# Loading gamma through GpSimd's DMA queue in a grouped instance norm

## Chip, cores, metric

The kernel runs on one core of a Trainium2 chip. The metric is the device time in microseconds (us), as a median over executions.

## The reference

```python
def setup_inputs():
    B, G, C_per_g, H, W = 4, 8, 16, 256, 256
    return {"x": np.random.randn(B, G, C_per_g, H, W).astype(np.float32),
            "gamma": np.random.randn(G, C_per_g).astype(np.float32)}

def reference(x, gamma):
    mu = x.mean(axis=(3, 4), keepdims=True)
    var = ((x - mu) ** 2).mean(axis=(3, 4), keepdims=True)
    x_norm = (x - mu) / np.sqrt(var + 1e-5)
    return (x_norm * gamma[None, :, :, None, None]).astype(np.float32)
```

Each of 512 channels of 65,536 values is normalized by its own mean and variance, and scaled by one of 128 gammas. That is 134 MB in and 134 MB out.

## The kernel before

The input is cut into 32 tiles of 128 rows by 8192 floats (4 MB). A tile holds 16 channels, each on 8 rows. There are six tile buffers ("slots"). Loads are issued by SyncE's queue, save two of the first six, and stores by ScalarE's queue.

```python
    def load(u, queue):
        queue.dma_start(out=slots[u % AHEAD][:], in_=xv[u])

    g_row = singles.tile([1, G * C], F32, name="g_row")
    for u in range(AHEAD):                                  # AHEAD = 6
        if u == 1:
            nc.scalar.dma_start(out=g_row[:], in_=gv[None, :])
        load(u, nc.scalar if u in (1, 3) else nc.sync)
    # ... cut: GpSimd writes eps, a one and the averaging matrix navg ...
    nc.vector.tensor_copy(out=g_rep[:], in_=g_row[:]...)     # each gamma eight times
    # ... cut: 8 small matmuls turn g_rep into columns ...
    nc.vector.tensor_copy(out=g_col[:], in_=g_ps[:])

    for u in range(U):                                      # U = 32
        t = slots[u % AHEAD]
        nc.vector.reduce_sum(out=st[:, u, 0:1], in_=t[:], axis=AX.X)
        square = nc.scalar.activation(out=junk[:], in_=t[:], func=ACTF.Square,
                                      accum_out=st[:, u, 1:2])
        # ... cut: matmul with navg, variance, root, reciprocal, times g_col ...
        nc.vector.tensor_scalar(out=t[:], in0=t[:], scalar1=ps[:, 0:1],
                                scalar2=scale[:, u : u + 1], op0=ALU.add, op1=ALU.mult)
        nc.scalar.dma_start(out=ov[u], in_=t[:])
        if u + AHEAD < U:
            load(u + AHEAD, nc.sync)
```

In the built program the transfers of SyncE and ScalarE have eight completion semaphores (counters that a transfer raises when it has landed) in turn. A transfer must wait until the last one on its semaphore has landed. In VectorE's order of instructions the copy of gamma stands in front of everything that it does with the first tile.

## Time and profile before

| | before |
|---|---|
| time, median of 3 | 627.18 us (626.75 to 627.25) |
| span of the profiled run | 625.2 us |
| mean DMA rate | 429 GB/s |

The busiest engines and how long a store takes to land, from the page's parts 1, 5 and 6. In part 5 the columns are busy time and mean ns of one, then the idle time before it and what ended it:

```profile
PE 21.4 (3%) x80; PEld 19.5 (3%) x80; DVE 443.2 (71%) x162; ACT 238.8 (38%) x98; POOL 1.3 (0%) x9
L103 DVE TENSOR_REDUCE st<-xt 128x1 f32<-128x8192 f32 x32 | 277.9, 8684 | 111.2 <-DMA xt<-in_x_dram 111.2
L126 DVE TENSOR_SCALAR xt<-xt,ps,scale 128x8192 f32<-128x8192 f32 x32 | 145.6, 4550 | 1.2
out_dram<-xt ACTq DMA_DIRECT2D x32, 4096.0 KB, 67.1
```

VectorE is the busiest engine but idles 111 us for loads. A store takes 67 us to land although 4 MB occupy the DMA engines for 9.6 us: it stands in a queue. Engines that wait for transfers, and transfers that wait for each other, point to the DMA engines as the bound.

### The profile page before, as it was taken

Reading aid. Unit: us, or ns where it says so; the run is one execution under the profiler, and the core shown is the slowest. Engines: PE = TensorE matmul, PEld = TensorE weight load, DVE = VectorE, ACT = ScalarE, POOL = GpSimd, SP = SyncE. Lnnn points to the kernel's source line nnn. Section 1 sums busy time; section 2 is a strip of 40 time slices with the busy share of each in tenths; the row PEclk is TensorE's granted clock in tenths of the full one; section 3 lists DMA queues with packets and bytes.
Section 4 is the critical chain, followed back from the end, with each engine's and each line's share of the span. In section 5 each row is a group of like instructions: output and inputs, shape, how many; then the busy total and the mean of one; then the engine's idle time right before and its main releaser. Section 6 shows DMA issues by size and latency. Waiting matters only on the chain.

```text
span 625.2 us, 626 instructions
## 1 busy us (share of the span) xinstructions
PE 21.4 (3%) x80; PEld 19.5 (3%) x80; DVE 443.2 (71%) x162; ACT 238.8 (38%) x98; POOL 1.3 (0%) x9
## 2 busy tenths in 40 slices
PE   2000000000000000000000000000000000000000
PEld 2000000000000000000000000000000000000000
DVE  0699999998867668676687766776667867668620
ACT  0444444444444224443244432344423443224400
POOL 0000000000000000000000000000000000000000
DMA  8999999999999999999999999999999999999998
GB/s 369 436 417 424 434 436 436 436 436 437 434 436 434 426 426 430 434 436 436 436 434 434 436 434 434 430 426 430 434 436 436 436 432 434 436 436 434 426 426 365
DMA packets 9220, 268.46 MB, mean 429 GB/s; under 512 B 1025, under 2 KB 1026, under 8 KB 1026
## 3 DMA queue, kind: packets, MB, share of 16 engines
q10 hardware_dynamic: 4898, 142.61, 52.8%
q1 hardware_dynamic: 4320, 125.83, 46.8%
q14 instruction: 2, 0.02, 0.0%
HBM read 134.22 MB, written 134.22 MB: 429 GB/s over the span
## 4 chain that ended last, share of the span: by engine, by line
another core or an unknown queue 64%; DMA 16%; DVE 13%; SPq 1%; PE 1%; issue 0%; ACT 0%
DMA xt<-in_x_dram 9%; DVE st L103 8%; DMA out_dram<-xt 7%; DVE xt L126 4%; SPq L48 1%; PE ps L112 1%; ACT std L117 0%; DVE nvar L113 0%; DVE rstd L121 0%; DVE scale L123 0%
## 5 line engine op out<-in xcount | busy, mean ns | idle before, releaser
L103 DVE TENSOR_REDUCE st<-xt 128x1 f32<-128x8192 f32 x32 | 277.9, 8684 | 111.2 <-DMA xt<-in_x_dram 111.2
L104 ACT ACTIVATE junk<-xt 128x8192 uint8<-128x8192 f32 x32 | 225.0, 7030 | 272.2 <-DMA xt<-in_x_dram 229.0
L126 DVE TENSOR_SCALAR xt<-xt,ps,scale 128x8192 f32<-128x8192 f32 x32 | 145.6, 4550 | 1.2
L117 ACT ACTIVATE std<-nvar,eps_t 128x1 f32<-128x1 f32 x32 | 9.4, 294 | 79.6 <-DVE nvar L113 79.6
L112 PE MATMUL ps<-st,navg 128*128 128x2 f32 x64 | 17.9, 349 | 568.0 <-DVE st L103 568.0
L112 PEld LDWEIGHTS ps<-st,navg 128*128 128x128 f32 x64 | 16.0, 312 | 569.8 <-issue 569.8
L113 DVE TENSOR_SCALAR nvar<-ps 128x1 f32<-128x1 f32 x32 | 9.2, 287 | 23.8 <-PE ps L112 23.8
L121 DVE RECIPROCAL rstd<-std 128x1 f32<-128x1 f32 x32 | 5.3, 164 | 11.6 <-ACT std L117 11.6
L104 ACT ACTIVATION_READ_ACCUMULATOR junk<-xt 128x1 f32 x32 | 6.0, 186 | 0.0
L123 DVE TENSOR_TENSOR scale<-rstd,g_col 128x1 f32<-128x1 f32 x32 | 5.1, 159 | 1.1
L84 PE MATMUL g_ps<-one,g_rep 1*128 1x1 f32 x16 | 3.5, 346 | 2.9 <-DVE g_rep L79 2.9
L84 PEld LDWEIGHTS g_ps<-one,g_rep 1*128 1x128 f32 x16 | 3.5, 325 | 2.9 <-POOL navg L68 2.9
L90 DVE COPY g_col<-g_ps 128x8 f32<-128x8 f32 x1 | 0.2, 166 | 3.7 <-PE g_ps L84 3.7
L74 ACT ACT_TABLE_LOAD x1 | 1.3, 1283 | 2.2 <-issue 2.2
L79 DVE COPY g_rep<-g_row 1x1024 f32<-1x1024 f32 x1 | 0.7, 681 | 2.1 <-DMA g_row<-in_gamma_dram 2.1
L64 POOL TENSOR_SCALAR_AFFINE_SELECT navg<-navg 128x128 f32<-128x128 f32 x1 | 0.4, 403 | 0.1
L68 POOL TENSOR_SCALAR_AFFINE_SELECT navg<-navg 128x128 f32<-128x128 f32 x1 | 0.4, 398 | 0.1
L63 POOL MEMSET navg<- 128x128 f32 x1 | 0.2, 220 | 0.0
L74 ACT ACTIVATE root_eps<-eps_t 128x1 f32<-128x1 f32 x1 | 0.2, 203 | 0.0
L147 POOL MEMSET const-bfloat16-1.0<- 128x1 bf16 x1 | 0.1, 101 | 0.0
L147 POOL MEMSET const-uint8-127<- 128x1 uint8 x1 | 0.1, 101 | 0.0
L147 POOL MEMSET const-float32-0.0<- 128x1 f32 x1 | 0.1, 98 | 0.3 <-issue 0.3
(3 smaller groups left out, 0.3 us busy)
## 6 DMA issues: line engine op xcount, KB each, us to landing
out_dram<-xt ACTq DMA_DIRECT2D x32, 4096.0 KB, 67.1
xt<-in_x_dram SPq DMA_DIRECT2D x30, 4096.0 KB, 33.8
xt<-in_x_dram ACTq DMA_DIRECT2D x2, 4096.0 KB, 33.3
g_row<-in_gamma_dram ACTq DMA_DIRECT2D x1, 0.5 KB
```

The costliest lines, as they stand in the source:

```text
L48: queue.dma_start(out=slots[u % AHEAD][:], in_=xv[u])
L74: nc.scalar.activation(out=root_eps[:], in_=eps_t[:], func=ACTF.Sqrt)
L79: nc.vector.tensor_copy(out=g_rep[:], in_=g_row[:].rearrange("o (n k) -> o n k", n=NG).unsqueeze(3).to_broadcast([1, NG, K, S]),)
L84: nc.tensor.matmul(out=g_ps[:, n : n + 1], lhsT=g_rep[:, n].rearrange("o k s -> o (k s)"), rhs=one[:], start=True, stop=True,)
L103: nc.vector.reduce_sum(out=st[:, u, 0:1], in_=t[:], axis=AX.X)
L104: square = nc.scalar.activation(out=junk[:], in_=t[:], func=ACTF.Square, accum_out=st[:, u, 1:2],)
L112: nc.tensor.matmul(out=ps[:], lhsT=navg_w, rhs=st[:, u], start=True, stop=True)
L113: nc.vector.tensor_scalar(out=nvar[:, u : u + 1], in0=ps[:, 0:1], scalar1=ps[:, 0:1], scalar2=ps[:, 1:2], op0=ALU.mult, op1=ALU.add,)
L117: nc.scalar.activation(out=std[:, u : u + 1], in_=nvar[:, u : u + 1], func=ACTF.Sqrt, bias=eps_t[:], scale=-1.0,)
L121: nc.vector.reciprocal(out=rstd[:, u : u + 1], in_=std[:, u : u + 1])
L123: nc.vector.tensor_mul(out=scale[:, u : u + 1], in0=rstd[:, u : u + 1], in1=g_col[:, g : g + 1],)
L126: nc.vector.tensor_scalar(out=t[:], in0=t[:], scalar1=ps[:, 0:1], scalar2=scale[:, u : u + 1], op0=ALU.add, op1=ALU.mult,)
```

## The change

The intent: 64 data transfers are a multiple of the eight semaphores, 65 are not. If gamma's load goes to GpSimd's queue, which has semaphores of its own, the data fill the eight evenly.

```diff
     g_row = singles.tile([1, G * C], F32, name="g_row")
+    nc.gpsimd.dma_start(out=g_row[:], in_=gv[None, :])
     for u in range(AHEAD):
-        if u == 1:
-            nc.scalar.dma_start(out=g_row[:], in_=gv[None, :])
         load(u, nc.scalar if u in (1, 3) else nc.sync)
```

## The prediction

> **What bounds the kernel now.** I read the share of busy time first, then the forty slices, then the stretches, and only then the waits. The header and the slices of the profile page:
>
> ```profile
> span 625.2 us, 626 instructions
> DMA  8999999999999999999999999999999999999998
> GB/s 369 436 417 424 434 436 436 436 436 437 434 436 434 426 426 430 434 436 436 436 434 434 436 434 434 430 426 430 434 436 436 436 432 434 436 436 434 426 426 365
> DMA packets 9220, 268.46 MB, mean 429 GB/s; under 512 B 1025, under 2 KB 1026, under 8 KB 1026
> ```
>
> The reader is to see that the DMA row is full from the second slice to the second last, while VectorE is at 71% and ScalarE at 38% of the span. The best slices move 436 GB/s. A slice is 625.2 / 40 = 15.63 us. Against 436 in each slice the forty rates fall short by 262 in sum (67 in the first, 71 in the last, 31 in the third and fourth together, 93 in all the rest), and 262 / 436 x 15.63 us = 9.4 us. So a change that made the transfers perfect from the first instant to the last could win 9.4 us, 1.5%. The stretches say where those are:
>
> ```profile
> 0.00:1.80 1.80, 0.00 (x0) 0.00 (x0) 0.00 (x0) 0.00 (x0) 1.07 (x9) 1.00 0.00 0
> 1.80:20.00 18.20, 3.54 (x16) 3.48 (x16) 0.85 (x2) 1.49 (x2) 0.22 (x1) 1.00 1.04 432
> 20.00:62.00 42.00, 1.67 (x6) 1.50 (x6) 38.15 (x15) 22.25 (x9) 0.00 (x0) 1.00 1.00 424
> 62.00:156.00 94.00, 3.36 (x12) 3.02 (x12) 85.73 (x31) 44.51 (x18) 0.00 (x0) 1.00 1.01 434
> 156.00:560.00 404.00, 11.71 (x42) 10.52 (x42) 290.79 (x105) 155.75 (x63) 0.00 (x0) 1.00 1.00 433
> 560.00:622.00 62.00, 1.12 (x4) 1.00 (x4) 27.69 (x10) 14.83 (x6) 0.00 (x0) 1.00 1.01 435
> 622.00:625.20 3.20, 0.00 (x0) 0.00 (x0) 0.00 (x0) 0.00 (x0) 0.00 (x0) 1.00 0.07 31
> ```
>
> The last two numbers of a row are the share of the sixteen DMA engines and GB/s. No byte moves before 1.8 us, the engines are full until 622.0, and the last 3.2 us are the tail. Between, the share is 1.00 or more in every stretch: no stage waits for an engine or a semaphore with idle transfers.
>
> The timeline shows the start, which is all that the change touches by intent:
>
> ```profile
> 0.80 1.90 SPq L48 DMA_DIRECT2D xt<-in_x_dram  x4
> 0.80 0.53 ACTq L54 DMA_DIRECT2D g_row<-in_gamma_dram  x1
> 1.37 0.84 ACTq L48 DMA_DIRECT2D xt<-in_x_dram  x2
> 2.06 0.68 DVE L79 COPY g_rep<-g_row 1x1024 f32<-1x1024 f32 x1 [2.06 <-DMA g_row<-in_gamma_dram]
> 6.46 0.17 DVE L90 COPY g_col<-g_ps 128x8 f32<-128x8 f32 x1 [3.72 <-PE g_ps L84]
> 20.32 8.69 DVE L103 TENSOR_REDUCE st<-xt 128x1 f32<-128x8192 f32 x1 [13.70 <-DMA xt<-in_x_dram]
> ```
>
> VectorE is done with gamma at 6.6 us and then idles 13.7 us for the first tile. And the semaphores, from the view of the load line and of the store line:
>
> ```profile
> L48 SPq EVENT_SEMAPHORE  x26: 28/18926/19472, 64.4 to 530.0; - x26
> L130 ACTq EVENT_SEMAPHORE  x27: 17/17/17, 74.9 to 573.2; - x27
> DMA to landing us min/median/max: 29.0/67.1/67.3
> ```
>
> These are minimum, median and maximum in ns, then the landing times of stores in us. The 26 waits on SyncE take about 19 us each: a load waits until the store of its slot has landed, which is real data dependence at the pace of the DMA. The 27 waits that ScalarE executes ahead of its stores take 17 ns, all of them: they were always met before ScalarE came to them.
>
> **What the Trainium skill says.** First, "DMA: Bandwidth & Descriptors", section "Issuing engines are not separate DMA queues": transfers started from scalar, sync or gpsimd run on the same 16 DMA engines, and starting them from several saves only the sequencer's issue time. The trace agrees as to the full engines; the issue time at stake is the 0.53 us above. Second, "Perfetto Trace Analysis", section "Roofline": a single active core is bounded by its 16 DMA engines at about 435 GB/s in sum; the 434 to 436 of most slices is that. Third, the DMA page's section "Why a DMA increments its semaphore by 16 and not by 1": a transfer whose slowest dimension is 128 rows spreads over 16 engines and each posts one increment, while a small one on fewer engines has the sequencer write the rest. The packet count agrees: 64 data transfers x 16 = 1024, and 1025 packets are under 512 B, so gamma had one data packet and one increment; its issue took 0.53 us against 0.34 us for a later store. Fourth, its section "Latency and other measured facts": first byte about 0.6 us on the HWDGE path (sync, scalar), about 1 us on the SWDGE path (gpsimd). No transfer from GpSimd is in this trace.
>
> **The change part by part.**
>
> One, ScalarE loses one issue, 0.53 us. Its two loads start at 0.80 instead of 1.37 us. Nothing is won: SyncE's first load was issued at 0.80 already and 4 MB occupy the engines for 4.19 / 0.436 = 9.6 us, so they have work from 1.8 us on either way. There is a small loss: the first tile shares the engines with the second, and loses its 0.57 us of lead, so it may land up to 0.6 us later (20.9 instead of 20.3). VectorE works tiles off in 14.93 us (35.34 to 50.27 in the chain of waits), the DMA needs 19.35 us for a load and a store, so this shift is swallowed by 157 us, where VectorE first waits for a tile again. Cost at the end: 0.
>
> Two, GpSimd gains one issue ahead of its memsets. I have no duration for it here. My estimate is that gamma lands at 3 to 8 us: issue at 0.80, the 1.3 us that gamma took on ScalarE's queue (0.80 to 2.06), the 0.4 us or more that the page's first byte is later, and some packets of 32 KB to wait behind (16 engines at 436 GB/s are 27 GB/s each, 1.2 us for one packet). The deadline: the first reduction at 20.32 must be preceded by the 0.68 us copy, the 3.7 us of small matmuls and the 0.17 us copy, 4.6 us in sum, so gamma may land as late as 15.7 us and nothing moves. The constants that GpSimd makes after it come later by its issue; the mean matrix is first needed at 29.1 us and eps at 20 us.
>
> Three, the semaphores. The built program of both shows which waits change. Before, the data transfers began at semaphore 1, gamma having 0; after the start, loads had the even ones and stores the odd ones, and the period is eight. Afterwards they begin at 0, loads have odd and stores even, and the period is eight still. In both, a store waits besides its data for the store four before it, and a load for the load four before it. The stores are spaced 4 x 19.35 = 77.4 us and land in at most 67.3 us: met 10 us early. Loads, at a median of 33.8 us, are met 43 us early. What vanishes is one wait, of the seventh load for gamma's semaphore, met 62 us before that load was issued at 64.5. What is new is that the third store waits for the fourth load, which is on the chip by then. Removed 0, added a few times 17 ns on ScalarE, which idles 62% of the span.
>
> Four, bytes. Gamma's 512 B split 16 ways are 32 small packets (16 of data, 16 of increments) instead of 2: two more short ones per engine, well under 0.1 us.
>
> Sum: 0 + 0 + 0 + under 0.1 us, off the path that sets the end save the last. The kernel stays at 1.8 us start, 620 us of full transfers, 3.2 us tail.
>
> **The rivals.** (a) The author's hope: uneven semaphores cost waits. Against it are the 17 ns waits and the DMA share of 1.00; for it only the slices of 417 and 424, where stores begin, and 426 to 430 later. If those came from a semaphore, the engines would idle in them, which they don't. All of it would be worth at most (31 + 93) / 436 x 15.63 = 4.4 us: 622.7. (b) Gamma lands late, since GpSimd's queue takes turns with two full queues, or its first issue is slow. If it passes 15.7 us by X, the first store at 35.4 us moves by X. But the six first loads alone fill the DMA to 1.8 + 6 x 9.6 = 59.4 us, so the engines would run dry only with X over 24 us, a landing past 40 us, and 2% (12.5 us) needs past 52. (c) The third queue costs something outside the transfers, in the start or the final drain: the time is 1.7 us above the span in the profiled run (626.89 against 625.2), and 1 or 2 us more would make 628 to 629. Nothing in the trace speaks for it; the program before declares GpSimd's queue too. (d) The first two loads, now started together, interleave otherwise and the rate in the first 60 us shifts: 424 against 434 there is 1 us in 42, either way.
>
> **Range and chances.** The prediction is the time before, 627.1 us. The three runs before spread by 0.5 us, and executions agree within 0.3%, 1.9 us. With (c) and (d) each worth about 1 us I take 625.7 to 628.4. Faster by 2% would need 614.6, under what the bytes allow at 436 GB/s (268.46 / 0.436 = 615.7 us), so only another chip or a mistake of mine gives it: 1%. Slower by 2% needs (b) at its worst or something unseen: 1%. Within 2%: 98%.
>
> **What would show it.** The DMA share stays at 1.00 from 1.8 to 622 us, and the mean at 429 GB/s. Packets are some 9250, with 1056 or so under 512 B, and a small third queue appears. ScalarE's first load is issued at 0.80 us. The copy of gamma starts at 3 to 8 us, and the first reduction at 20.3 to 20.9 us. SyncE's waits stay at 19 us and ScalarE's at 17 ns. I would be wrong if the first reduction started after 25 us, if a stretch had idle DMA, if ScalarE's waits ahead of stores took microseconds, or if the gap between time and span grew past 3 us.

## The result

| | before | after |
|---|---|---|
| median of 6 | 627.05 us | 626.92 us |
| range | 626.75 to 627.38 | 626.73 to 627.32 |
| profiled span | 625.2 us | 625.2 us |

The ratio is 0.9999, with a 95% interval of 0.9986 to 1.0012: the same. (A ratio here is the mean time of one kernel's fast runs over that of the other's fast runs of the same rounds, so not quite the ratio of the medians.)

The page of the changed kernel, its rates, packets and the new queue:

```profile
span 625.2 us, 627 instructions
GB/s 369 436 403 436 436 436 436 436 426 432 434 434 436 424 434 436 436 434 436 436 421 434 434 434 432 432 434 436 436 434 436 436 419 434 434 436 432 432 434 369
DMA packets 9251, 268.46 MB, mean 429 GB/s; under 512 B 1057, under 2 KB 1057, under 8 KB 1057
q0 software_dynamic: 32, 0.00, 0.0%
g_row<-in_gamma_dram POOLq DMA_DIRECT2D x1, 0.5 KB, 9.3
```

The mean rate is 429 GB/s again. The dips below 436 have moved to other slices but add up to nearly the same (265 against 262). Queue q0 is GpSimd's, with gamma's 32 small packets. The last line says that gamma took 9.3 us to land.

The start in the timeline (start us, duration us, engine, line, what; in brackets the idle time before it and what ended it):

```profile
0.81 0.89 ACTq L48 DMA_DIRECT2D xt<-in_x_dram  x2
1.29 0.61 POOL L52 DMA_DIRECT2D g_row<-in_gamma_dram  x1 [0.78 <-POOLq L146]
10.64 0.68 DVE L78 COPY g_rep<-g_row 1x1024 f32<-1x1024 f32 x1 [10.64 <-DMA g_row<-in_gamma_dram]
15.05 0.17 DVE L89 COPY g_col<-g_ps 128x8 f32<-128x8 f32 x1 [3.73 <-PE g_ps L83]
22.76 8.69 DVE L102 TENSOR_REDUCE st<-xt 128x1 f32<-128x8192 f32 x1 [7.55 <-DMA xt<-in_x_dram]
```

ScalarE's first load is issued at 0.81 instead of 1.37 us. Gamma is there at 10.6 instead of 2.1 us. The first reduction starts at 22.76 instead of 20.32 us. So the work on the first tile began 2.4 us later, and the end did not move. The stretches show why (the last two numbers are DMA share and GB/s):

```profile
20.00:62.00 42.00, 1.66 (x6) 1.51 (x6) 36.20 (x11) 21.96 (x8) 0.00 (x0) 1.00 1.00 424
156.00:560.00 404.00, 11.73 (x42) 10.54 (x42) 290.20 (x106) 155.75 (x63) 0.00 (x0) 1.00 1.00 433
622.00:625.20 3.20, 0.00 (x0) 0.00 (x0) 0.00 (x0) 0.00 (x0) 0.00 (x0) 1.00 0.26 113
```

The DMA engines are as full as before, at the same 424 and 433 GB/s. The last stretch carries 113 instead of 31 GB/s, 0.26 MB more or 0.6 us of transfers, and ends at the same time.

One more reading, which the prediction had missed. Of each tile I compared the end of VectorE's last pass with the issue of the tile's store. Of 32 stores, 31 are issued 0.03 or 0.04 us later. The 28th is not, in either kernel. The timeline before:

```profile
515.83 4.55 DVE L126 TENSOR_SCALAR xt<-xt,ps,scale 128x8192 f32<-128x8192 f32 x1
524.76 0.34 ACTq L130 DMA_DIRECT2D out_dram<-xt  x1
```

And after:

```profile
518.55 4.55 DVE L125 TENSOR_SCALAR xt<-xt,ps,scale 128x8192 f32<-128x8192 f32 x1
527.49 0.34 ACTq L129 DMA_DIRECT2D out_dram<-xt  x1
```

The tile is ready at 515.83 + 4.55 = 520.38 us, and the store goes out at 524.76: held for 4.38 us (4.39 after). In the built program the 28th store waits for the semaphore of the 29th load. When the loads have run out, the last stores take over the loads' semaphores, and this happens with 64 transfers as with 65.

### The profile page after: what moved, and what is told of

It is laid out like the page before. It is cut to its first block, busy times and chain, and to the rows that moved or that the text cites. A ratio compares the mean times of both kernels' runs of the same rounds, so it can differ in the third digit from the quotient of the medians.

```text
span 625.2 us, 627 instructions
## 1 busy us (share of the span) xinstructions
PE 21.4 (3%) x80; PEld 19.6 (3%) x80; DVE 443.2 (71%) x162; ACT 238.8 (38%) x98; POOL 1.9 (0%) x10
## 2 busy tenths in 40 slices
DMA packets 9251, 268.46 MB, mean 429 GB/s; under 512 B 1057, under 2 KB 1057, under 8 KB 1057
## 4 chain that ended last, share of the span: by engine, by line
another core or an unknown queue 61%; DMA 17%; DVE 15%; SPq 1%; PE 1%; issue 0%; ACT 0%
DMA xt<-in_x_dram 10%; DVE st L102 10%; DMA out_dram<-xt 8%; DVE xt L125 5%; SPq L48 1%; PE ps L111 1%; ACT std L116 0%; DVE nvar L112 0%; DVE rstd L120 0%; DVE scale L122 0%
## 5 line engine op out<-in xcount | busy, mean ns | idle before, releaser
L78 DVE COPY g_rep<-g_row 1x1024 f32<-1x1024 f32 x1 | 0.7, 683 | 10.6 <-DMA g_row<-in_gamma_dram 10.6
```

The lines of the kernel that those rows point to most:

```text
L78: nc.vector.tensor_copy(out=g_rep[:], in_=g_row[:].rearrange("o (n k) -> o n k", n=NG).unsqueeze(3).to_broadcast([1, NG, K, S]),)
```

## The experiments

Theory: the bytes set the time; gamma's queue, the start and the semaphores all lie beside transfers that keep the DMA engines full. Rivals: (A) semaphore waits cost time, so evenness matters; (B) a gain (ScalarE's earlier start) and a cost (a third queue, gamma's lateness) cancel; (C) VectorE's start counts.

**Gamma on ScalarE's queue, behind its loads**

```diff
-    nc.gpsimd.dma_start(out=g_row[:], in_=gv[None, :])
     for u in range(AHEAD):
         load(u, nc.scalar if u in (1, 3) else nc.sync)
+    nc.scalar.dma_start(out=g_row[:], in_=gv[None, :])
```

> Gamma goes back to ScalarE's queue, but behind its two loads: no third queue, and ScalarE's first load starts at 0.8 us as in the changed kernel. My theory (the bytes set the time; the start is swallowed): same time as before, 626.5 to 627.6 us, and the first reduction at about 22.8 us as in the changed kernel, because it is the lost head start of the first load that delays the first tile, not GpSimd's queue. Rival 'uneven semaphores cost': 65 transfers share eight semaphores, so no faster than before and slower than the changed kernel. Rival 'a gain and a cost cancel' (third queue costs X, ScalarE's earlier start wins X): faster than both by X. If GpSimd's queue delays the first tile, the first reduction is at 20.3 us.

Measured: 633.92 us (633.51 to 635.27), ratio 1.0109 (1.0094 to 1.0124). My expectation of the time missed, and so did rival B's, which wanted a gain. It is slower than the changed kernel, as rival A wanted, but A knows of no reason for 7 us over the kernel before, which has 65 transfers too. The first reduction missed as well. The timeline and the stretches of this run:

```profile
1.72 0.54 ACTq L54 DMA_DIRECT2D g_row<-in_gamma_dram  x1
44.34 0.68 DVE L78 COPY g_rep<-g_row 1x1024 f32<-1x1024 f32 x1 [44.34 <-DMA g_row<-in_gamma_dram]
48.84 8.67 DVE L102 TENSOR_REDUCE st<-xt 128x1 f32<-128x8192 f32 x1
```

```profile
58.00:64.00 6.00, 0.21 (x2) 0.13 (x1) 5.31 (x5) 0.29 (x1) 0.00 (x0) 1.00 0.41 175
64.00:70.00 6.00, 0.00 (x0) 0.00 (x0) 6.00 (x1) 5.70 (x1) 0.00 (x0) 1.00 1.02 437
70.00:76.00 6.00, 0.56 (x2) 0.50 (x2) 4.82 (x5) 1.72 (x3) 0.00 (x0) 1.00 0.61 262
```

512 bytes issued at 1.72 us landed at 44.3 us: they queued behind the two 4 MB loads of the same queue, which share the engines with SyncE's. VectorE began at 48.84 us, the first store went out at 63.88 us, and the six first loads were done by about 60. The engines then idled 0.59 x 6 + 0.39 x 6 = 5.9 us, most of the 7.0 us lost. This is the prediction's rival (b), a late gamma, in a place where I hadn't looked for it. In the changed kernel gamma waits only 9.3 us, on a queue that holds nothing else, though the same six loads are under way. That the order of issue is not what counts is seen in a later run: issued by GpSimd at 24.0 us, behind all six loads, it landed 8.7 us later (60 memsets).

**GpSimd's queue, and an idle copy of gamma ahead on ScalarE's**

```diff
     for u in range(AHEAD):
+        if u == 1:
+            g_idle = singles.tile([1, G * C], F32, name="g_idle")
+            nc.scalar.dma_start(out=g_idle[:], in_=gv[None, :])
         load(u, nc.scalar if u in (1, 3) else nc.sync)
```

> The changed kernel, plus a copy of gamma that ScalarE loads ahead of its first tile and nobody reads: the head start of the first load is back, and the third queue stays. My theory: 626.5 to 627.6 us, and the first reduction back at 20.3 us. Rival 'a gain and a cost cancel': slower than before by X, since it has the cost alone. If GpSimd's queue delays the first tile, the first reduction stays at 22.8 us.

Measured: 627.0 us, ratio 0.9997 (0.9985 to 1.001). Its timeline:

```profile
10.66 0.68 DVE L81 COPY g_rep<-g_row 1x1024 f32<-1x1024 f32 x1 [10.66 <-DMA g_row<-in_gamma_dram]
20.36 8.69 DVE L105 TENSOR_REDUCE st<-xt 128x1 f32<-128x8192 f32 x1 [5.13 <-DMA xt<-in_x_dram]
```

Gamma is as late as in the changed kernel, and yet the first reduction is back at 20.36 us. So the 2.4 us come from the order of the first two loads, not from GpSimd's queue. Rival B wanted a cost here and found none.

**Two idle copies ahead** (the same edit, twice over)

> The changed kernel with two idle copies of gamma on ScalarE ahead of its first load, so that SyncE's first load has 1.1 us of head start instead of 0.57 or 0. The first reduction started at 22.76 us without a head start and at 20.36 with 0.57 us, a step of 2.4 us, two packets of 32 KB at 1.2 us each. If the head start counts in whole packets already under way or fetched, it comes at 20.3 less zero to two more steps of 1.2 us (20.3, 19.1 or 17.9); if the tile only gains what it was ahead in time, at 19.8. The time 626.5 to 627.6 us in every case.

Measured: first reduction at 20.30 us; 627.25 us, ratio 1.0002 (0.9984 to 1.002). ScalarE's first load was issued at 1.64 us, a head start of 0.83 us (I had reckoned 1.1), and brought nothing over the one of 0.57. So between 0.57 and 0.83 us the gain no longer grows; how it grows between 0 and 0.57 us was not tried. That its 2.4 us are two packets of 32 KB is a guess that fits, not shown.

**No gamma at all** (VectorE writes ones; wrong result)

```diff
-    nc.gpsimd.dma_start(out=g_row[:], in_=gv[None, :])
+    nc.vector.memset(g_row[:], 1.0)
```

> No load of gamma at all (VectorE writes ones in its place; a wrong result on purpose): 64 transfers of data alone on the eight semaphores, no third queue. My theory: 626.5 to 627.6 us, first reduction at 22.8 us. Both rivals expect it to be the fastest: 'uneven semaphores cost' and 'the gamma load costs something in either place' both want a gain over before, clear of the 0.13% of the interval, that is under 626.2 us.

Measured: 627.02 us, ratio 0.9996 (0.9982 to 1.001); first reduction at 22.78 us. Gamma's load costs nothing measurable in either place, and 64 transfers alone on eight semaphores are no faster than 65. This speaks against A and B directly.

**The transfers alone** (no arithmetic on the tiles; each store waits for its load; wrong result)

```diff
     for u in range(U):
         t = slots[u % AHEAD]
-        nc.vector.reduce_sum(...)          # and all that follows, to the last pass
         nc.scalar.dma_start(out=ov[u], in_=t[:])
```

> No arithmetic on the tiles: each store waits for its load alone and writes the input back (a wrong result on purpose). All 64 transfers, gamma on GpSimd as in the changed kernel. My theory: the engines' work costs nothing, so 624 to 627.5 us. If anything but the transfers is on the path (compute, the start of VectorE, waits for VectorE), it falls towards the 615.7 us of the bytes at 436 GB/s plus 1.8 us of start and about 5 us of tail and outside the span, 622 us or less.

Measured: 626.41 us (626.27 to 626.43), ratio 0.9985 (0.9972 to 0.9998). Two of its stretches:

```profile
20.00:62.00 42.00, 0.00 (x0) 0.00 (x0) 0.00 (x0) 0.00 (x0) 0.00 (x0) 1.00 1.00 424
156.00:560.00 404.00, 0.00 (x0) 0.00 (x0) 0.00 (x0) 0.00 (x0) 0.00 (x0) 1.00 1.00 433
```

All the arithmetic together costs 0.15%, about 0.9 us. The slower stretch of 424 GB/s is there without any arithmetic, so it belongs to the transfers. With this pattern of transfers neither kernel has more than about 1 us to win (1.8 us at the far end of the interval), which is why no faster version was tried.

**Gamma late: 60 memsets ahead of it**

```diff
-    nc.gpsimd.dma_start(out=g_row[:], in_=gv[None, :])
     ...
+    idle = singles.tile([P, 256], F32, name="idle")
+    for _ in range(60):
+        nc.gpsimd.memset(idle[:], 0.0)
+    nc.gpsimd.dma_start(out=g_row[:], in_=gv[None, :])
```

> GpSimd issues gamma after 60 idle memsets, which I estimate at 0.3 us each: it should land at about 30 us instead of 10.6, and hold up VectorE (first reduction at about 35 us, 12 us later than in the changed kernel). My theory: the six first loads fill the DMA until 59.4 us, and the first store is issued some 20 us after gamma lands, at about 50, in time: 626.5 to 628 us. Rival 'VectorE's start counts': about 12 us more, 639 us.

Measured: 627.54 us (627.43 to 629.61, the highest being the profiled one), ratio 1.0003 (0.9988 to 1.0018). Gamma was there at 32.7 us and the first reduction started at 37.2, 14.5 us later than in the changed kernel, and the time did not move. Rival C wanted 639 us.

**Gamma later: 150 memsets**

> The same with 150 memsets: gamma should land at 55 to 60 us. My theory: the DMA runs dry from 59.4 us until the first store is issued, 20 us after gamma lands; the time grows by about the landing time minus 39.7 us, some 15 to 22 us: 642 to 650 us, with a stretch of DMA share near zero just before the first store. Rival 'VectorE's start counts in full': 45 us more than the changed kernel, 672 us. Rival 'the start never counts': 627 us.

Measured: 650.98 us, ratio 1.0381 (1.0365 to 1.0397), 24.0 us more, and 1 us above my range. Gamma was there at 61.9 us. The stretches:

```profile
58.00:64.00 6.00, 1.23 (x6) 1.26 (x7) 0.68 (x1) 0.00 (x0) 0.00 (x0) 1.00 0.41 175
64.00:82.00 18.00, 2.87 (x13) 2.73 (x13) 14.47 (x7) 0.42 (x2) 0.00 (x0) 1.00 0.00 0
```

The DMA engines have nothing to do until the first store at 81.5 us: 0.59 x 6 + 18 = 21.5 us idle, and the rest in the stretch after. The rule "landing time less 39.7 us" gives 22.2 us here and 4.6 us for gamma at 44.3 us; measured were 24.0 and 7.0. It finds the place where the start begins to count, and is 2 us short both times.

**Two tiny loads per tile on SyncE's queue, so that the semaphores come round sooner**

```diff
+        for k in range(2):
+            i = u * 2 + k
+            nc.sync.dma_start(out=tiny[:, i : i + 1], in_=gv[None, 0:1])
         nc.scalar.dma_start(out=ov[u], in_=t[:])
```

> The changed kernel with two loads of 4 bytes per tile on SyncE's queue, which nobody reads: the eight semaphores now come round every two tiles, so each store waits for the store two before it, not four. Stores land after 62 us and are 19.35 us apart, so this wait must bind: ScalarE's waits ahead of stores grow from 17 ns to many us. My theory: the DMA still has two stores and one or two loads to work at, the share stays at 1.00, and the time at 627 to 633 us (what the 64 tiny transfers themselves cost included). Rival 'semaphore waits cost time': 32 stores held up by some us each, 650 us or more.

**Six tiny loads per tile** (the same with `range(6)`; in these runs the line that makes `tiny` is cut)

> The same with six tiny loads per tile: the semaphores come round with every tile, and each store waits for the one before it to land, each load too. One store and one load in flight. My theory: the DMA runs dry where both pause together, for about 2 us at most per tile, so the time is between 630 and 690 us, and the DMA share falls below 1.00 by just as much as the time grows. Rival 'semaphore waits cost time': much more than in the run with two, in proportion to ScalarE's waits, over 700 us.

Measured: with two, 659.06 to 667.25 us in the three fast runs (median of all four 665.28), ratio 1.0572 (1.0523 to 1.0622). With six, 682.51 us (677.89 to 684.08), ratio 1.0868 (1.0831 to 1.0905). My expectation for two was plainly wrong, and rival A's number came out, but not its picture of 32 held stores: in the next run, which has the same two tiny loads until the end and a fast profile, the fifth to eleventh stores are held 3.7 to 6.5 us, but those from the 14th to the 27th only the usual 0.03 or 0.04 us. So waits that bind do cost, but the stores' are not the only ones. With six, each store is held 5.8 to 9.9 us through the middle, and SyncE's loads are held too. The middle of the run with six, then what SyncE's loads waited for in the changed kernel and in this run (us in total, times, longest):

```profile
156.00:560.00 404.00, 11.63 (x40) 10.00 (x40) 270.12 (x97) 148.04 (x59) 0.00 (x0) 1.00 0.99 409
SPq L48 <- DMA out_dram<-xt: 534.7, 26, 59.8
SPq L48 <- DMA xt<-in_x_dram: 417.4, 26, 19.5
```

In the changed kernel a load waits for the store that empties its slot, here for the load before it. With six the time lay in my range, but the mechanism that I gave held in part only. At 409 instead of 433 GB/s the middle lost 22 us at a DMA share of 0.99: a busy share is not a rate, for a packet was then under way for 1.27 us on average (0.99 x 16 x 32,768 B / 409 GB/s) instead of 1.21. After 560 us the share was 0.81 and then 0.69, 31 us of idle engines. The end, in the timeline of the run with six (a fast one; the profile of the run with two is of its slowest execution):

```profile
582.51 4.55 DVE L126 TENSOR_SCALAR xt<-xt,ps,scale 128x8192 f32<-128x8192 f32 x1
591.74 21.48 SPq L132 DMA_DIRECT2D tiny<-in_gamma_dram  x36
611.69 0.34 ACTq L133 DMA_DIRECT2D out_dram<-xt  x1
612.08 7.03 ACT L104 ACTIVATE junk<-xt 128x8192 uint8<-128x8192 f32 x1 [29.99 <-DMA tiny<-in_gamma_dram]
```

The 28th tile is ready at 587.06 us. Its store is held for 24.63 us, until 611.69, by a semaphore that a tiny load now carries. ScalarE issues in order, so its next square waits 30 us behind that store. Then four tiles are worked off one by one, 14.9 us each with nothing to overlap, at 296 GB/s.

**Two tiny loads per tile, but none at the end**

```diff
-        for k in range(2):
+        for k in range(2 if u + AHEAD < U else 0):
```

> The run with two tiny loads per tile came out 38 us slower, against my expectation. My reading of its trace: the holds of 4 to 6 us in the middle cost little (the DMA moved 423 instead of 433 GB/s there, some 9 us), and most was lost after 560 us, where the 28th store was held for 36.65 us by tiny loads queued behind the last tiles, with ScalarE stuck in front of its remaining four squares. Here the tiny loads stop with the last load, nothing else is changed. If that reading is right: 632 to 645 us, the 28th store held for less than 15 us. If holds in the middle are what costs, or the tiny loads themselves: still 655 us or more.

Measured: the three fast runs 641.94, 644.38 and 651.41 us (a fourth, slow, 652.23), ratio 1.0312 (1.0242 to 1.0382). Two of the three lie in my range, the third above it. The 28th store was still held, for 14.7 us. So the tiny loads at the end account for part of the loss, some 17 us between the means of the fast runs (663.2 and 645.9), and the trace says where most of the rest is: between 156 and 560 us the rate was 426 instead of 433 GB/s, which is 6.5 us, and after 610 us the DMA share was 0.70 and less, 10 us of idle engines where the kernel before has 3. In the middle no store was held after the 13th; 23 of SyncE's 26 loads waited for an earlier load, 387 us in sum.

**The tiny transfers on GpSimd's queue**

```diff
-            nc.sync.dma_start(out=tiny[:, i : i + 1], in_=gv[None, 0:1])
+            nc.gpsimd.dma_start(out=tiny[:, i : i + 1], in_=scale[0:1, u : u + 1])
```

> A control for the runs with tiny transfers: again two of 4 bytes per tile, but issued by GpSimd (copied from VectorE's scale of the tile, so that each comes in its tile's time), whose semaphores are its own. The stores' and loads' semaphores come round every four tiles as in the changed kernel. If it was the waits (each store for the store two before it, and the 28th for tiny loads) that cost 38 and 21 us in the two runs with tiny loads on SyncE's queue: 626.5 to 628 us here, and no store held but the 28th by 4.4 us. If the tiny transfers themselves cost in the engines' queues: 635 us or more, with no store held.

Measured: 628.34 us (627.9 to 628.41), ratio 1.0018 (1.0004 to 1.0031). No store was held but the 28th, by 4.42 us. The 64 tiny transfers and their 2048 further packets cost about 1.1 us by the ratio (1.4 by the medians), a little over my expectation, and not the 19 or 36 us that the fast executions lost with two on SyncE's queue. SyncE's loads waited for stores again. So on SyncE's queue it is the waits and the queue's order that cost, not the transfers as such; the two were not separated. One difference remains: these tiny transfers copy from `scale` on the chip and not from gamma in memory.

**The 28th store freed**

```diff
         if u + AHEAD < U:
             load(u + AHEAD, nc.sync)
+        elif u + AHEAD > U:
+            nc.sync.dma_start(out=tiny[:, u : u + 1], in_=scale[0:1, u : u + 1])
```

> In both kernels the 28th store is held for 4.4 us by its semaphore (it waits for the 29th load, since the loads have run out and the stores take over the loads' semaphores). Here five copies of 4 bytes stand in for the missing loads, so that this store goes back to the semaphore of the store four before it. My theory (the bytes set the time): the hold shrinks to the 0.03 us of the other stores, and the time stays at 626.5 to 627.6 us, since three stores are queued in front and the 29th tile is not there before that moment anyway. Rival 'that wait costs': 622.6 us or so, 4.4 us less.

Measured: 627.01 us, ratio 1.0 (0.9988 to 1.0013). No store was held any more, the 28th included. The one wait for a semaphore in its turn that holds a store in both kernels costs nothing: the next tile lands at that very moment, and other stores are in the queue.

## Why the prediction was right

- **The bound.** It held as argued. The transfers without arithmetic take 626.41 us, and the 424 GB/s between 20 and 62 us belong to them. One sum was wrong: the 9.4 us that perfect transfers could win. The row GB/s counts whole packets: 13 packets of 32 KB on each of 16 engines in 15.63 us are 436, and 12 are 403, the third slice of the changed kernel. The rate that is kept up is the 433 of the 404 us stretch. At 433 the 268.46 MB need 620.0 us, and the DMA engines were full for 620.2. So the dips in the row are mostly the counting, and little but the two ends, 1.8 and 3.2 us, was left to win.
- **ScalarE's earlier load wins nothing.** Right. The size of the side effect was wrong: the first reduction came 2.44 us later, not up to 0.6. The step that failed is "shares the engines with the second, and loses its 0.57 us of lead": the lead is worth 2.4 us, at 0.57 and at 0.83 us alike, as the runs with one and two idle copies show. It was swallowed as said.
- **Gamma's landing.** The estimate of 3 to 8 us was short; it was usable at 10.6. The term that was too small is most likely the wait behind large packets: gamma took 8.7 to 9.4 us with the loads under way and 4.8 when they were nearly done. The deadline of 15.7 us was kept, with 5 us to spare.
- **Rival (b), the late gamma.** Its limit, about 40 us, was confirmed on both sides: 32.7 us cost nothing, 44.3 cost 7 us, 61.9 cost 24 us.
- **The semaphores.** The conclusion held: an even filling wins nothing. One step was wrong. "They were always met before ScalarE came to them" does not hold for the 28th store, held 4.4 us in both kernels: it does not wait for "the store four before it" but for the 29th load. The reading was at fault: ScalarE's waits show 17 ns also in the run where that store was held 24.6 us. What shows a hold is the gap between the end of VectorE's pass and the store's issue.
- **What is open:** why the first tile's lead counts as 2.4 us; why gamma takes 9.3 us on a queue of its own; and why a packet takes longer in the middle of the runs where loads wait for loads.

## What to carry to other kernels

When the DMA engines are full from the first to the last microsecond, first ask what the transfers alone take; that number says how much any rearrangement can win, and here it was about 1 us. A small transfer that something waits for belongs ahead of the big ones or on a queue that holds none: behind two 4 MB loads it cost 7 us. Extra transfers on the shared semaphores are not free because they are small: when they shortened the turn of the semaphores from four tiles to two or one, 5.7 and 8.7% were lost, and 3.1% when they stopped with the last load.

## What the Trainium skill lacked or had wrong

- "DMA: Bandwidth & Descriptors", section "Latency and other measured facts", gives a first byte of about 1 us for GpSimd's path and 0.6 us for the other. What counts here is what else is under way: the 512 bytes took 9.3 us from GpSimd with both other queues full, 4.8 us when the six first loads were nearly done (the run with 150 memsets), 1.3 us to use as the first transfer on ScalarE's queue, and 42.6 us behind two loads of 4 MB on that queue. The page has 2 us at high load for the access to memory alone, and no time for a small transfer that others are ahead of.
- "Perfetto Trace Analysis", section "Per-instruction lifecycle", says that semaphore waits lie outside the profiled window. ScalarE agrees: 17 ns where a store was held for 24.6 us. SyncE's waits ahead of loads show durations of 18.9 us, so there a part of the wait was inside. The built programs say when: an instruction that waits for one semaphore showed 17 ns always (ScalarE's, and that of the changed kernel's seventh load, which the first store held until 62.6 us); one that waits for two, as SyncE's others do, showed the wait for the second of them only, 18.9 us where that was the store's and 28 ns where the store's came first (every fourth load of the kernel before). The page doesn't have this.
- No page has what the framework's turn of eight semaphores does at the end of a kernel, when one kind of transfer runs out and the other takes over its semaphores: the 28th store held for 4.4 us here without cost, and for 14.7 to 24.6 us at a cost with tiny loads in the turn.
